# Five gate projections in 512-wide pairs, with new homes for two of the gate tiles, in a two-layer hybrid trunk kernel

## The chip, the core and the metric

The kernel runs on one core of a Trainium2 chip. A core has five engines with an instruction stream each: TensorE (PE in the profile) multiplies matrices and writes its sums into PSUM, VectorE (DVE) and ScalarE (ACT) do elementwise work and are the ones that read PSUM here, GpSimd (POOL) does a little elementwise work, and SyncE (SP) starts most of the transfers from memory. The engines run side by side and wait for each other by semaphores, each in the order of its own stream. The metric is the time of one execution on the device, in microseconds (us).

## What is computed

There are 256 positions of width 1024 and two layers. Each layer normalises its input, projects it by one weight matrix into ten pieces, runs three branches, multiplies each branch by a SiLU gate, projects the concatenation back and adds it to the input. A last normalisation ends the program. All is float32 (the kernel works with products of rounded halves, see below).

```python
def hybrid_layer(x, ...):
    hn = rms_norm(x, norm_gain)
    proj = einsum('bsd,de->bse', hn, w_in)
    a_q, a_k, a_v, a_g, b_x, b_g, c_q, c_k, c_v, c_g = split(proj)
    y_a = dilated_attention(rope(a_q), rope(a_k), a_v) * silu(a_g)     # width 512, 8 heads
    y_b = rg_lru_branch(b_x, ...) * silu(b_g)                          # width 256, a scan over time
    y_c = stick_breaking_attention(c_q, c_k, c_v) * silu(c_g)          # width 256, 4 heads
    y = concatenate([y_a, y_b, y_c])
    return x + einsum('bse,ed->bsd', y, w_out)
```

## The kernel before

**Precision by halves.** TensorE multiplies in a rounded float32 form, so each float operand is kept as a rounded half and a remainder: weights as `whi` and `wlo`, the normalised input as `xh` and `xl`. A product is whi·xh + whi·xl + wlo·xh. `xh` and `xl` lie side by side in one tile `xx`. The weights arrive in chunks of 256 output columns: `load_chunk` (L102) starts two transfers, then ACT rounds four pieces of 512 columns into `whi` (L115) and DVE subtracts four remainders into `wlo` (L117). `weights(l, c)` hands out a chunk and asks for the one two places on. Four chunks can be held at a time.

**Two ways to project a chunk.** `proj_b` (L326) computes the 256 outputs of a chunk in two halves of 128, for all 256 positions. Unpaired (L353, helper `mm3`, L225), both halves go into one PSUM bank, and each half is 24 matmuls with 256 columns: 8 of whi·xh, 8 of whi·xl, 8 of wlo·xh. Paired (L336 to L351), a half has a bank of its own: 8 matmuls with the 512 columns of `xx` (L344) give whi·xh and whi·xl side by side, and 8 with 256 columns (L341) add wlo·xh. Afterwards ACT copies the right part of the bank into a tile `low` (L347), and DVE adds it to the left part (L349) into `to`, a tile in SBUF that the caller names, or a scratch tile. The first half begins with its 512-wide matmuls, the second with its 256-wide ones. The table `PAIRED` (L46) says which chunks of which layer are paired: in before none of layer 0, and seven of layer 1.

**Banks.** The pool `pp` has three PSUM banks. A bank is free again when the instructions that read it are done. `at` has four others (tiles `s`), `yp` one (tile `y`).

**The order of the work around the gates.** The code of a layer from L654 on runs: the stick-breaking gate chunk CG; the turning of the softmaxed scores of dilated heads 0 to 3; the recurrence's gate chunk BG, between whose halves the function `third` stands (recurrence gates, stick-breaking values and their `emit_y`, values of dilated heads 0 to 3 into a `pp` bank that is kept as `y_c["y"]`, scores of heads 4 to 7); the recurrence's scan `lru_scan` and its `emit_y`; the softmax of heads 4 to 7; the first dilated gate AG; `emit_y` of heads 0 to 3, which frees the bank of `y_c["y"]`; the second dilated gate AG+1; and the output projection. `silu` (L423) applies the gate: in layer 0 DVE first scales the sums by the row norms (L413, reading the sums' bank), then ACT takes the sigmoid (L429) and DVE multiplies (L430). `emit_y` multiplies a branch by its gate (L434), rounds (L436, `yh`) and subtracts (L437, `yl`). The rows of `w_out` are packed in the order `yk`, so that block k of the products `ys` meets its weights.

**The output projection** (from L682) sums over eight blocks of `ys`, first blocks 0 to 3 (`ys[0]`: recurrence and stick-breaking) for four output tiles, then blocks 4 to 7. In layer 1 one output tile is started on a bank that still holds the leftover of AG+1 (`seeded`), into which ACT writes a part of the residual (L692).

PE's stream has the order of the code. The streams of the other engines are ordered by a scheduler when the program is built, so a row of the code may come later there than it stands. Names in the rows below: `pp_`, `s_`, `y_` are PSUM banks, `scr_` scratch tiles, `pr_` softmax probabilities, `den_` their denominators, `th_`, `it_`, `rt_`, `av_` tiles of the recurrence.

Of the kernel before, what the change touches and what calls it, by code (L numbers as in the profile page):

```python
# [9 lines left out]
F32 = mybir.dt.float32  # L10
# [5 lines left out]
P = 128  # L16
S = 256
# [25 lines left out]

CH_AV, CH_CV, CH_CQ, CH_CK, CH_BX, CH_CG, CH_BG, CH_AG, CH_O = 0, 2, 3, 4, 7, 10, 11, 12, 14
CH_AQ, CH_AK = (5, 8), (6, 9)
PAIRED = ((), (CH_CQ, CH_CK, CH_AQ[0], CH_AK[0], CH_BX, CH_AQ[1], CH_AK[1]))  # L46


@with_exitstack
def trunk_kernel(ctx: ExitStack, tc: tile.TileContext, x, first_x, first, wpack, prm_d, gatew, gains, consts, rope, out):  # L50
# [6 lines left out]
    sb = ctx.enter_context(tc.tile_pool(name="sb", bufs=1))  # L57
    wk = ctx.enter_context(tc.tile_pool(name="wk", bufs=2))
    pp = ctx.enter_context(tc.tile_pool(name="pp", bufs=3, space=bass.MemoryType.PSUM))
# [3 lines left out]
    def bank(pool, tag):  # L63
        return pool.tile([P, 512], F32, name=tag, tag=tag)

    def scr(w):
        return wk.tile([P, 512], F32, name="scr", tag="scr", bufs=SCR)[:, 0:w]
# [3 lines left out]
    def dep(inst, on):  # L71
        tc.add_manual_dep(inst.ins, on.ins.name, nosync)
        return inst
# [3 lines left out]
    def table(name, behind=()):  # L77
        load = act.preload_act_table_set(name)  # L78
        for u in (*loaded["users"], *behind):
            dep(load, u)  # L80
        loaded["load"], loaded["users"] = load, []
# [6 lines left out]
    def v2(a, n=2):  # L88
        return a.rearrange("p (b t) -> p b t", b=n)
# [40 lines left out]
    def weights(l, c, ahead=AHEAD):  # L130
        ask(l, c, ahead)
        return ready.pop((l, c))
# [16 lines left out]
    for k in range(NK):  # L149
# [10 lines left out]
        w = st[:, S:1024]  # L160
# [67 lines left out]
    last = {}  # L228
# [82 lines left out]
    for l in range(L):  # L311
# [14 lines left out]
        def proj_b(c, mid=None, to=None, sc=1.0):  # L326
            pair = c in PAIRED[l]
            hi, lo = [a.rearrange("p (k c) -> p k c", c=256) for a in weights(l, c, AHEAD - 1 if mid else AHEAD)]
            if pair:
                flat = None if to is not None else scr(512)  # L330
                to = [v2(flat)[:, b, :] for b in range(2)] if to is None else to
            else:
                flat = bank(pp, "pp")
            for b in range(2):
                cs = slice(b * P, b * P + P)
                if pair:  # L336
                    ps = bank(pp, "pp")
                    seq = [(b ^ i, k) for i in range(2) for k in range(NK)]
                    for i, (is_lo, k) in enumerate(seq):
                        if is_lo:  # L340
                            pe.matmul(ps[:, 0:S], lo[:, k, cs], xh[:, k, :], start=i == 0, stop=i == len(seq) - 1,  # L341
                                      skip_group_check=True)
                        else:
                            pe.matmul(ps, hi[:, k, cs], xx[:, k].rearrange("p h t -> p (h t)"), start=i == 0,  # L344
                                      stop=i == len(seq) - 1, skip_group_check=True)
                    low = wk.tile([P, S], F32, name="low", tag="low", bufs=2)
                    act.activation(low, ps[:, S:2 * S], AF.Copy, scale=sc)  # L347
                    if sc == 1.0:
                        dve.tensor_add(to[b], ps[:, 0:S], low)  # L349
                    else:  # L350
                        dve.scalar_tensor_tensor(to[b], ps[:, 0:S], sc, low, ALU.mult, ALU.add)  # L351
                else:
                    mm3(flat[:, b * 256:(b + 1) * 256], [lambda k, a=a: a[:, k, cs] for a in (hi, lo)],  # L353
                        [lambda k, a=a: a[:, k, :] for a in (xh, xl)], range(NK), b == 0, True, True)
                if b == 0 and mid:
                    mid()
                    ask(l, c)
            return flat

        def proj_to(dst, c, mid=None, sc=1.0):  # L360
            if l > 0 and c in PAIRED[l]:
                proj_b(c, mid, [dst[:, b, :] for b in range(2)], sc)
# [40 lines left out]
        vc = sb.tile([P, NT, 256], F32, name="vc", tag="vc")  # L403
# [19 lines left out]
        def silu(dst, ps):  # L423
            sg = v2(scr(512))
            src = v2(ps)
            if l == 0:
                src = v2(scr(512))
                scaled(src, ps)
            tab(sg, src, AF.Sigmoid)  # L429
            dve.tensor_mul(dst, src, sg)  # L430

        def emit_y(src, gate, k0, n):
            dst = v2(scr(n * S), n)
            dve.tensor_mul(dst, src, gate)  # L434
            yh, yl = [v[:, k0 % 4:k0 % 4 + n, :] for v in ys[k0 // 4]]
            act.activation(yh, dst, AF.Copy)  # L436
            dve.tensor_sub(yl, dst, yh.bitcast(F32))  # L437
# [4 lines left out]
        def values(vt, wts, h0, y=None):  # L442
            y = bank(yp, "y") if y is None else y
            for p in (0, 2):
                for s0, o in ((0, 0), (1, 128)):
                    for i in (p, p + 1):
                        hr, _, hs = head(h0 + i)
                        pe.matmul(y[hr, p * 128 + o:p * 128 + 256], vt[:, s0, hs], wts[i][s0],  # L448
                                  start=s0 == 0, stop=s0 == 1)
            return v2(y)  # L450
# [122 lines left out]
        rt = sb.tile([P, 2, S], F32, name="rt", tag="rt")  # L573
        it = sb.tile([P, 2, S], F32, name="it", tag="it")
        th = sb.tile([P, 2, S], F32, name="th", tag="th")
        bg = sb.tile([P, 2, S], F32, name="bg", tag="bg")
        cg = sb.tile([P, 2, S], F32, name="cg", tag="cg")
# [61 lines left out]
        sw_t, sw_heads = turned_tile()  # L639
# [20 lines left out]

        def third():
            lru_gates()
            emit_y(values(vc, sw_heads, 0), cg, 2, 2)
            y_c["y"] = values(va, pts, 0, bank(pp, "pp"))
            y_c["s"] = dil_scores(4)

# [1 line left out]
        y_half(1)  # L668
        table(LN_EXP)
        lru_scan()  # L670
        emit_y(rt, bg, 0, 2)
        dil_softmax(y_c["s"])
        ag = sb.tile([P, 4, S], F32, name="ag", tag="ag")
        ps = proj_b(CH_AG)
        table(SIGM)
        silu(ag[:, 0:2, :], ps)
        emit_y(y_c["y"], ag[:, 0:2, :], 4, 2)
        seeded = proj_b(CH_AG + 1)
        silu(ag[:, 2:4, :], seeded)
        table(LN_EXP)  # L680

        def out_mm(ps, w, t, half, ks, first, last, c0=0, c1=512, skip=False):  # L682
            v = [a.rearrange("p (k c) -> p k c", c=512) for a in w]
            ts_ = slice(t * P, t * P + P)
            mm3(ps, [lambda k, a=a: a[:, k, ts_] for a in ys[half]],
                [lambda k, a=a: a[:, k, c0:c1] for a in v], ks, first, last, skip)

        o_ps = {}
# [4 lines left out]
        for n2 in range(2):  # L693
            w = weights(l, CH_O + n2)
            for t in range(NT):
                if l > 0 and (t, n2) == (1, 1):
                    tail = [(bank(yp, "y")[:, 0:LATE], 0, LATE), (seed, LATE, 512)]
                    for ps, c0, c1 in tail[::-1]:
                        out_mm(ps, w, t, 0, range(4), c0 == 0, False, c0, c1, c0 > 0)
                    continue  # L700
                o_ps[t, n2] = bank(at, "s") if (t, n2) == (0, 0) else bank(pp, "pp")
                out_mm(o_ps[t, n2], w, t, 0, range(4), True, False)
                if (t, n2) == (0, 0):
                    y_c["p"] = dil_transposes(4)
                if (t, n2) == (0, 1):
                    emit_y(values(va, y_c["p"], 4), ag[:, 2:4, :], 6, 2)
# [57 lines left out]
def _pack_weights(w_in, w_out):  # L764
    wp = np.empty((L, NCH, P, 2048), np.float32)
    narrow = ((CH_CV, 3072), (CH_BX, 2048), (CH_BG, 2304), (CH_AG, 1536), (CH_AG + 1, 1792), (CH_CG, 3328),
              (CH_CQ, 2560), (CH_CK, 2816), (CH_AQ[0], 0), (CH_AQ[1], 256), (CH_AK[0], 512), (CH_AK[1], 768))
    yk = (4, 5, 6, 7, 0, 1, 2, 3)
    for l in range(L):
        wi = w_in[l].reshape(NK, P, 3584)  # L770
        for h in range(2):
            wp[l, CH_AV + h] = wi[4 * h:4 * h + 4, :, 1024:1536].transpose(1, 0, 2).reshape(P, 2048)
        for c, col in narrow:
            blk = wi[:, :, col:col + 256]
            if c in CH_AQ + CH_AK:
                blk = blk.reshape(NK, P, 4, 2, 32).transpose(0, 1, 3, 2, 4).reshape(NK, P, 256)
            wp[l, c] = blk.transpose(1, 0, 2).reshape(P, 2048)
        wo = w_out[l].reshape(NK, P, D)
        for h in range(2):
            for n in range(2):  # L780
                blk = np.stack([wo[k, :, n * 512:n * 512 + 512] for k in yk[4 * h:4 * h + 4]])
                wp[l, CH_O + 2 * h + n] = blk.transpose(1, 0, 2).reshape(P, 2048)
    return wp
# [56 lines left out]
```

## Time and profile before

| what | us |
|---|---|
| median of 3 runs (lowest, highest) | 245.55 (245.23, 247.58) |
| the profiled execution, its own time | 246.08 |
| its span, from first to last instruction | 244.2 |
| DVE busy, of the span | 195.7 (80%) |
| ACT busy, of the span | 171.5 (70%) |

The views of the profile that are quoted below have these forms. A row of the timeline has a start, a duration, an engine, the source line, the operation, output<-input, the shape and a count: equal instructions that follow each other are one row. Matmuls overlap at their ends, so what a row costs PE is the time from its start to the next row's start. A row of the list of waits has the waiting engine and line, whom it waited for, the total, the count and the longest. A row by windows has the window, its length, the busy time (and count) of PE, PE's weight loads, DVE, ACT and POOL, the clock granted to TensorE as a share of the full one, the share of DMA, and GB/s.

### The profile page before, as it was taken

Reading aid. Unit: us, or ns where it says so; the run is one execution under the profiler, and the core shown is the slowest. Engines: PE = TensorE matmul, PEld = TensorE weight load, DVE = VectorE, ACT = ScalarE, POOL = GpSimd, SP = SyncE. Lnnn points to the kernel's source line nnn. Section 1 sums busy time; section 2 is a strip of 40 time slices with the busy share of each in tenths; the row PEclk is TensorE's granted clock in tenths of the full one; section 3 lists DMA queues with packets and bytes.
Section 4 is the critical chain, followed back from the end, with each engine's and each line's share of the span. In section 5 each row is a group of like instructions: output and inputs, shape, how many; then the busy total and the mean of one; then the engine's idle time right before and its main releaser. Section 6 shows DMA issues by size and latency. Waiting matters only on the chain.

```text
span 244.2 us, 4755 instructions
## 1 busy us (share of the span) xinstructions
PE 237.5 (97%) x1747; PEld 212.1 (87%) x1747; DVE 195.7 (80%) x468; ACT 171.5 (70%) x372; POOL 11.3 (5%) x43
## 2 busy tenths in 40 slices
PE   8999999999999999999999999999999999999991
PEld 4788999999998899878888888888889889987881
DVE  4794789999999888986594675999999967885262
ACT  4669989628688499974663775876579749993143
POOL 0037100002000000000000000000010000000000
PEclk9999999999999999999999999999999999999997
DMA  7989989455836832277358388606470762000013
GB/s 211 395 262 386 381 274 309 167 192 182 274 120 217 300 112 77 87 217 274 113 154 262 114 268 269 212 15 191 156 215 27 238 257 86 0 3 0 0 53 121
DMA packets 14038, 43.90 MB, mean 180 GB/s; under 512 B 1728, under 2 KB 3008, under 8 KB 14016
## 3 DMA queue, kind: packets, MB, share of 16 engines
q1 hardware_dynamic: 13248, 42.43, 51.6%
q10 hardware_dynamic: 576, 0.66, 0.7%
q0 software_dynamic: 192, 0.52, 0.7%
q8 instruction: 14, 0.23, 0.4%
q14 instruction: 8, 0.07, 0.1%
HBM read 42.03 MB, written 1.05 MB: 176 GB/s over the span
## 4 chain that ended last, share of the span: by engine, by line
PE 94%; DMA 3%; ACT 1%; SPq 0%; issue 0%; DVE 0%; DVEq 0%
PE pp L225 48%; PE pp L344 10%; PE s L225 9%; PE pp L341 6%; PE s L181 4%; PE s L484 3%; DMA st<-first 3%; PE y L448 2%; PE pp L383 2%; PE s L537 2%; PE pp L181 2%; PE s L464 1%; PE y L225 1%; PE pp L448 1%; PE s L596 1%; PE s L273 1%
## 5 line engine op out<-in xcount | busy, mean ns | idle before, releaser
L117 DVE TENSOR_TENSOR wlo<-st,whi 128x512 fp32r<-128x512 f32 x128 | 81.6, 682 | 9.1 <-ACT whi L115 8.7
L115 ACT ACTIVATE whi<-st 128x512 fp32r<-128x512 f32 x130 | 72.5, 627 | 13.0 <-PE pp L225 6.8
L225 PE MATMUL pp<-xx,whi 128*128 128x256 f32 x480 | 63.6, 285 | 0.0
L225 PEld LDWEIGHTS pp<-xx,whi 128*128 128x128 f32 x480 | 59.7, 191 | 1.3 <-issue 0.3
L225 PE MATMUL pp<-xx,wlo 128*128 128x256 f32 x240 | 33.7, 283 | 0.0
L225 PEld LDWEIGHTS pp<-xx,wlo 128*128 128x128 f32 x240 | 31.0, 192 | 0.0
L344 PE MATMUL pp<-xx,whi 128*128 128x512 f32 x112 | 27.2, 392 | 0.0
L344 PEld LDWEIGHTS pp<-xx,whi 128*128 128x128 f32 x112 | 20.5, 188 | 3.9
L84 ACT ACTIVATE pr<-scr,mn 128x128 f32<-128x128 f32 (+1 forms) x32 | 14.1, 442 | 6.6 <-DVE mn L544 6.6
L78 ACT ACT_TABLE_LOAD x13 | 16.7, 1283 | 1.9 <-PEq L833 1.7
L341 PEld LDWEIGHTS pp<-xx,wlo 128*128 128x128 f32 x112 | 14.5, 191 | 1.0 <-ACT scr L84 0.3
L341 PE MATMUL pp<-xx,wlo 128*128 128x256 f32 x112 | 15.3, 285 | 0.0
L225 PE MATMUL pp<-whi,yh 128*128 128x512 f32 (+1 forms) x48 | 13.3, 382 | 0.0
L225 PE MATMUL pp<-wlo,yh 128*128 128x512 f32 (+1 forms) x48 | 12.8, 372 | 0.0
L225 PE MATMUL pp<-whi,yl 128*128 128x512 f32 (+1 forms) x48 | 12.8, 372 | 0.0
L181 PE MATMUL s<-whi,xx 128*128 128x512 f32 (+1 forms) x36 | 9.8, 392 | 0.4 <-ACT whi L167 0.4
L436 ACT ACTIVATE yh<-scr 128x512 fp32r<-128x512 f32 x8 | 5.1, 632 | 7.2 <-DVE scr L434 7.1
L225 PEld LDWEIGHTS pp<-whi,yl 128*128 128x128 f32 x48 | 8.6, 188 | 1.6
L225 PEld LDWEIGHTS pp<-wlo,yh 128*128 128x128 f32 x48 | 8.6, 188 | 1.6
L225 PEld LDWEIGHTS pp<-whi,yh 128*128 128x128 f32 x48 | 8.3, 188 | 1.6 <-issue 0.3
L544 DVE CUSTOM_DVE_ANT_0 scr<-s,con 128x128 f32<-128x128 f32 (+1 forms) x32 | 9.2, 350 | 0.0
L347 ACT ACTIVATE low<-pp 128x256 f32<-128x256 f32 x14 | 5.3, 378 | 5.5 <-PE pp L344 4.7
(188 smaller groups left out, 368.4 us busy)
## 6 DMA issues: line engine op xcount, KB each, us to landing
st<-w_pack SPq DMA_DIRECT2D x66, 512.0 KB, 5.3
st<-first SPq DMA_DIRECT2D x7, 512.0 KB, 6.3
xres<-x_in SPq DMA_DIRECT2D x4, 256.0 KB, 6.9
gw_t<-gate_w SPq DMA_DIRECT2D x2, 256.0 KB, 6.4
gn<-gains SPq DMA_DIRECT2D x2, 256.0 KB, 5.7
xs<-xc POOLq DMA_DIRECT2D x4, 128.0 KB, 4.3
gf<-gains SPq DMA_DIRECT2D x2, 256.0 KB, 6.0
out<-st ACTq DMA_DIRECT2D x2, 192.0 KB, 2.6
```

Of the source, the lines that this page charges most:

```text
L78: load = act.preload_act_table_set(name)
L84: i = dep(act.activation(*a, **k), loaded["load"])
L115: split[l, c] = act.activation(h, part, AF.Copy)
L117: dve.tensor_sub(r, part, h.bitcast(F32))
L181: pe.matmul(ps[t][:, c0:c1], a[:, k, t * P:(t + 1) * P], b, start=k == 0 and all(m[0] is not ps for m in seq[:i]), stop=k == NK - 1 and al ...
L225: pe.matmul(ps, a(k), b(k), start=first and i == 0, stop=last and i == len(seq) - 1, skip_group_check=skip)
L341: pe.matmul(ps[:, 0:S], lo[:, k, cs], xh[:, k, :], start=i == 0, stop=i == len(seq) - 1, skip_group_check=True)
L344: pe.matmul(ps, hi[:, k, cs], xx[:, k].rearrange("p h t -> p (h t)"), start=i == 0, stop=i == len(seq) - 1, skip_group_check=True)
L347: act.activation(low, ps[:, S:2 * S], AF.Copy, scale=sc)
L448: pe.matmul(y[hr, p * 128 + o:p * 128 + 256], vt[:, s0, hs], wts[i][s0], start=s0 == 0, stop=s0 == 1)
L484: pe.transpose(tp[:, i * P:(i + 1) * P], tiles[h0 + h][:, j * P:(j + 1) * P], ident)
L544: dve.tensor_tensor_reduce(xs[:, cs], sps[h][:, cs], nmask[:, cs], -0.125, 3e38, ALU.add, ALU.min, mn[:, t:t + 1])
```

## The change

The change pairs five more chunks: CG, BG, AG and AG+1 of layer 1, and AG+1 of layer 0. In layer 1 the sums of AG go into a tile `agf` in the place that the gate of the stick-breaking branch (`cg`) had, and AG is called ahead of the softmax of heads 4 to 7. The leftover bank of layer 1 (`seeded`) is now the one of the second half of AG+1. The stick-breaking product becomes block 0 and 1 of `ys`, the recurrence's block 2 and 3 (with `w_out` packed to suit), and the first four blocks of an output tile are multiplied in two groups of two blocks.

```diff
-PAIRED = ((), (CH_CQ, CH_CK, CH_AQ[0], CH_AK[0], CH_BX, CH_AQ[1], CH_AK[1]))
+PAIRED = ((CH_AG + 1,), (CH_CQ, CH_CK, CH_AQ[0], CH_AK[0], CH_BX, CH_AQ[1], CH_AK[1], CH_CG, CH_BG, CH_AG, CH_AG + 1))
...
                 if pair:
-                    ps = bank(pp, "pp")
+                    ps = last["bank"] = bank(pp, "pp")
...
             lru_gates()
-            emit_y(values(vc, sw_heads, 0), cg, 2, 2)
+            emit_y(values(vc, sw_heads, 0), cg, 0, 2)
...
         lru_scan()
-        emit_y(rt, bg, 0, 2)
+        emit_y(rt, bg, 2, 2)
+        ag = sb.tile([P, 4, S], F32, name="ag", tag="ag")
+        ps = None
+        if CH_AG in PAIRED[l]:
+            agf = sb.tile([P, 2, S], F32, name="agf", tag="cg")
+            proj_b(CH_AG, None, [agf[:, b, :] for b in range(2)])
+            ps = agf.rearrange("p b t -> p (b t)")
         dil_softmax(y_c["s"])
-        ag = sb.tile([P, 4, S], F32, name="ag", tag="ag")
-        ps = proj_b(CH_AG)
+        ps = proj_b(CH_AG) if ps is None else ps
         table(SIGM)
         silu(ag[:, 0:2, :], ps)
         emit_y(y_c["y"], ag[:, 0:2, :], 4, 2)
         seeded = proj_b(CH_AG + 1)
         silu(ag[:, 2:4, :], seeded)
+        if CH_AG + 1 in PAIRED[l]:
+            seeded = last["bank"]
...
                 o_ps[t, n2] = bank(at, "s") if (t, n2) == (0, 0) else bank(pp, "pp")
-                out_mm(o_ps[t, n2], w, t, 0, range(4), True, False)
+                for ks in ((0, 1), (2, 3)):
+                    out_mm(o_ps[t, n2], w, t, 0, ks, ks[0] == 0, False)
...
-    yk = (4, 5, 6, 7, 0, 1, 2, 3)
+    yk = (6, 7, 4, 5, 0, 1, 2, 3)
```

PE in layer 0, before: AG (`pp_1352`), AG+1 in one bank (`pp_1425`), the first output tile.

```order
L225 MATMUL pp_1352<-xx_81,whi_1042 128x256 x16
L225 MATMUL pp_1352<-xx_81,wlo_1043 128x256 x8
L225 MATMUL pp_1425<-xx_81,whi_1247 128x256 x16
L225 MATMUL pp_1425<-xx_81,wlo_1248 128x256 x8
L225 MATMUL pp_1425<-xx_81,whi_1247 128x256 x16
L225 MATMUL pp_1425<-xx_81,wlo_1248 128x256 x8
L225 MATMUL s_1494<-whi_1338,yh_1130 128x512 x4
```

The same place with the change: AG+1 has a bank for each half, `pp_1426` and `pp_1446`.

```order
L225 MATMUL pp_1352<-xx_81,whi_1042 128x256 x16
L225 MATMUL pp_1352<-xx_81,wlo_1043 128x256 x8
L344 MATMUL pp_1426<-xx_81,whi_1247 128x512 x8
L341 MATMUL pp_1426<-xx_81,wlo_1248 128x256 x8
L341 MATMUL pp_1446<-xx_81,wlo_1248 128x256 x8
L344 MATMUL pp_1446<-xx_81,whi_1247 128x512 x8
L225 MATMUL s_1486<-whi_1338,yh_1130 128x512 x2
```

When `pp_1446` is asked for, two of the three banks are taken by `y_c["y"]` and by `pp_1426`, so it is the bank of `pp_1352`, and its first matmul waits for the DVE instruction that reads `pp_1352`.

DVE in layer 0, before, from the recurrence's scan to that reader (L413) and on.

```order
L618 SCALAR_TENSOR_TENSOR rt_329<-av_1293,it_330 128x256 x2
L557 TENSOR_SCALAR pr_1323<-pr_1323,den_1324 128x128
L434 TENSOR_TENSOR scr_1305<-rt_329,bg_332 128x512
L557 TENSOR_SCALAR pr_1323<-pr_1323,den_1324 128x256
L555 RECIPROCAL den_1331<-den_1331 128x2
L413 SCALAR_TENSOR_TENSOR scr_1403<-pp_1352,rb_289 128x512
L557 TENSOR_SCALAR pr_1330<-pr_1330,den_1331 128x128
L437 TENSOR_TENSOR yl_1131<-scr_1305,yh_1130 128x512
```

The same with the change.

```order
L618 SCALAR_TENSOR_TENSOR rt_329<-av_1293,it_330 128x256 x2
L557 TENSOR_SCALAR pr_1324<-pr_1324,den_1325 128x128
L434 TENSOR_TENSOR scr_1305<-rt_329,bg_332 128x512
L557 TENSOR_SCALAR pr_1324<-pr_1324,den_1325 128x256
L555 RECIPROCAL den_1332<-den_1332 128x2
L413 SCALAR_TENSOR_TENSOR scr_1403<-pp_1352,rb_289 128x512
L557 TENSOR_SCALAR pr_1331<-pr_1331,den_1332 128x128
L437 TENSOR_TENSOR yl_1131<-scr_1305,yh_1130 128x512
```

The reader of `pp_1352` stands in the same row of DVE's stream in both, behind the recurrence's scan.

ACT in layer 1, before, from the rounding of the second output chunk (`whi_2821`) and BG's sigmoid (L84) to the recurrence's logarithm (`th_1848`).

```order
L115 ACTIVATE whi_2821<-st_2823 128x512 x2
L84 ACTIVATE scr_2699<-pp_2546 128x512
L78 ACT_TABLE_LOAD
L84 ACTIVATE av_2705<-rt_1846,c8_285 128x256 x2
L84 ACTIVATE pr_2721,den_2722<-scr_2645,mn_2646 128x128
L84 ACTIVATE pr_2721,den_2722<-scr_2645,mn_2646 128x256
L84 ACTIVATE pr_2728,den_2729<-scr_2649,mn_2650 128x128
L84 ACTIVATE pr_2728,den_2729<-scr_2649,mn_2650 128x256
L84 ACTIVATE th_1848<-scr_2709,tiny_281 128x512
```

The same with the change: `low_2672` is of BG's second half, `low_2730` and `low_2750` are of AG's halves.

```order
L347 ACTIVATE low_2672<-pp_2655 128x256
L115 ACTIVATE whi_2789<-st_2791 128x512 x2
L84 ACTIVATE scr_2675<-scr_2530 128x512
L78 ACT_TABLE_LOAD
L84 ACTIVATE av_2681<-rt_1838,c8_285 128x256 x2
L347 ACTIVATE low_2730<-pp_2713 128x256
L84 ACTIVATE pr_2753,den_2754<-scr_2625,mn_2626 128x128
L84 ACTIVATE pr_2753,den_2754<-scr_2625,mn_2626 128x256
L84 ACTIVATE pr_2760,den_2761<-scr_2629,mn_2630 128x128
L84 ACTIVATE pr_2760,den_2761<-scr_2629,mn_2630 128x256
L84 ACTIVATE th_1840<-scr_2685,tiny_281 128x512
L347 ACTIVATE low_2750<-pp_2733 128x256
```

The three copies stand among the recurrence's steps and the exponentials, and BG's sigmoid now reads a tile that DVE fills (`scr_2530`) in place of the bank.

## The prediction

> **What bounds the kernel now.** I read the engines' shares on the page first, then PE's list of waits, then PE's timeline around the changed chunks, and only then the timelines of DVE and ACT there.
>
> ```profile
> PE 237.5 (97%) x1747; PEld 212.1 (87%) x1747; DVE 195.7 (80%) x468; ACT 171.5 (70%) x372; POOL 11.3 (5%) x43
> ```
>
> ```profile
> PE y L147 <- DVE cold L135: 1.2, 1, 1.2
> PE s L181 <- ACT whi L167: 0.4, 1, 0.4
> ```
>
> PE is busy for 97% of the span, and its whole list of waits is two rows, both from the first ten microseconds. From there to the output PE goes from matmul to matmul without a hole. So the kernel has one price list. A microsecond less of PE work is a microsecond gained, a microsecond in which PE waits is a microsecond lost, and nothing later can give it back, since there is no later wait that it could shorten. Work on ACT and DVE costs nothing until PE waits for it.
>
> **What pairing saves.** PE's timeline has the same chunk size in both forms: AG+1 of layer 0, unpaired, and a chunk of layer 1 that is paired already.
>
> ```profile
> 91.66 2.08 PE L225 MATMUL pp<-xx,whi 128*128 128x256 f32 x16
> ...
> 97.42 1.09 PE L225 MATMUL s<-whi,yh 128*128 128x512 f32 x4
> ...
> 144.23 3.82 PE L344 MATMUL pp<-xx,whi 128*128 128x512 f32 x16
> 147.88 2.08 PE L341 MATMUL pp<-xx,wlo 128*128 128x256 f32 x16
> 149.80 3.82 PE L344 MATMUL pp<-xx,whi 128*128 128x512 f32 x16
> ```
>
> From start to start the unpaired chunk takes 97.42 - 91.66 = 5.76 us for 48 matmuls, 120 ns each. The paired one takes 149.80 - 144.23 = 5.57 us: 16 wide ones in 3.65 (228 ns each) and 16 narrow ones in 1.92. The same columns pass through the array; a wide matmul saves only about 11 ns against two narrow ones. That is 0.19 us per chunk, and a paired half is 1.83 + 0.96 = 2.79 us.
>
> [...]
>
> Layer 1, from PE's timeline (the row at 189.93 ends CG, the one at 202.31 begins AG, the one at 213.83 ends AG+1):
>
> ```profile
> 184.07 2.17 PE L225 MATMUL pp<-xx,whi 128*128 128x256 f32 x16
> ...
> 189.93 1.48 PE L484 MATMUL s<-con,pr 128*128 128x128 f32 x12
> ...
> 202.31 2.08 PE L225 MATMUL pp<-xx,whi 128*128 128x256 f32 x16
> ...
> 213.83 1.09 PE L225 MATMUL s<-whi,yh 128*128 128x512 f32 x4
> ```
>
> CG takes 5.86 us and will take 5.57: 0.29 saved. BG's halves stand among other work and save half of 0.19 each: 0.19. AG and AG+1 take 11.52 and will take 11.14: 0.38. Layer 1 saves 0.86 us, at the least nothing and at the most 1.2 (four chunks at CG's 0.29).
>
> **What pairing costs in layer 0.** A pair needs two banks where one did. The second half of AG+1 gets the bank of AG's sums, and those are read by DVE's L413, which stands behind the recurrence's scan. DVE's timeline there:
>
> ```profile
> 93.39 0.69 DVE L616 TENSOR_TENSOR it<-it,th 128x512 f32<-128x512 f32 x1 [0.54 <-ACT th L84]
> ...
> 95.48 0.68 DVE L434 TENSOR_TENSOR scr<-rt,bg 128x512 f32<-128x512 f32 x1
> ...
> 96.42 0.67 DVE L413 SCALAR_TENSOR_TENSOR scr<-pp,rb 128x512 f32<-128x512 f32 x1
> 97.01 0.27 DVE L557 TENSOR_SCALAR pr<-pr,den 128x128 f32<-128x128 f32 x1
> ```
>
> AG is finished on PE at 91.66, but its sums are read from 96.42 to 97.09, since DVE works through its stream in order and the scan ahead of L413 waits for ACT's exponential of `th`. In before nobody needed this bank so soon: all of AG+1 went into another one. Now PE does the first half of AG+1 from 91.66 to 94.45 and then needs the bank. Nothing ahead of L413 is touched by the change, so it still ends at 97.09. PE waits 2.6 us and does the second half until 97.13 + 2.87 = 100.0 (its first group after a pause is taken 0.08 longer). AG+1 ended at 97.42 before, so layer 0 loses 2.6 us, its 0.19 of saving already counted. The bounds are narrow, since all rows exist: 2.4 if the bank is given up with the next DVE row at 97.01 and the half takes 2.79; 2.9 if the handover costs 0.3. Everything behind waits for PE and moves along. ACT's and DVE's two copies and two adds are done while PE waits or has its next matmuls.
>
> **What pairing costs in layer 1.** Four chunks bring eight ACT copies and eight DVE adds. The question is whether a bank or a `yh` comes too late. The tightest place is the first half of AG+1, which needs the bank of AG's first half. ACT's timeline, the price of a copy, and DVE's row behind the recurrence's exponentials `av`:
>
> ```profile
> 184.36 0.37 ACT L347 ACTIVATE low<-pp 128x256 f32<-128x256 f32 x1
> ```
>
> ```profile
> 201.55 1.16 ACT L115 ACTIVATE whi<-st 128x512 fp32r<-128x512 f32 x2 [2.66 <-PE pp L225]
> 202.61 0.58 ACT L84 ACTIVATE scr<-pp 128x512 f32<-128x512 f32 x1
> 203.21 1.28 ACT L78 ACT_TABLE_LOAD   x1
> 204.50 0.91 ACT L84 ACTIVATE av<-rt,c 128x256 f32<-128x256 f32 x2
> ```
>
> ```profile
> 205.44 0.69 DVE L612 TENSOR_TENSOR scr<-av 128x512 f32<-128x512 f32 x1 [0.98 <-ACT av L84]
> ```
>
> On the clock of before, less what CG and BG save (0.48), BG ends on PE at 201.83. Its copy begins about 0.3 later (the copy at 184.36 follows a PE handover near 184.07) and takes 0.26 to the next start, an estimate from its 0.37 less the overlap of neighbouring rows: 202.4. Behind it the two roundings take 1.06 (201.55 to 202.61), the sigmoid 0.6, the table 1.29: `av` begins at 205.35, 0.85 later than before. DVE's L612 follows 0.94 behind, at 206.3, takes 0.6, and then the add that frees the bank takes 0.4: 207.3. PE wants the bank at 201.83 + 5.57 = 207.40. That fits by 0.1 us, so I take 0.1 for waits in layer 1, between 0 and 0.6 (a bank late by half a microsecond, a shade more elsewhere). The recurrence's `yh` is late by some 1.2 us in all, but the reordered output projection covers it: its first six matmuls (1.4 us at 228 ns) now multiply stick-breaking blocks, which are long there, where before the first one needed the recurrence.
>
> Edits with one answer. Splitting the first blocks of an output tile into two groups leaves the number and size of its matmuls. The leftover bank only changes its name. `agf` takes the place of `cg`, whose last reader is the product before AG. The order of SP's and POOL's transfers stays the same, so calling AG ahead of the softmax moves no load.
>
> **The sum.** -0.86 + 2.6 + 0.1 = +1.8 us. The profiled execution took 246.08 us (span 244.2) and would take 247.9. It stood 0.5 above the median of 245.55, on which I put the forecast: 247.4 us, +0.7%.
>
> **The rivals.** *Slower: the wait takes TensorE's clock with it.* The end of the run shows how the granted clock answers to idleness: PE's last row, and three windows behind it.
>
> ```profile
> 238.48 0.64 PE L225 MATMUL pp<-whi,yl 128*128 128x256 f32 x4
> ```
>
> ```profile
> 241.00:241.10 0.10, 0.00 (x0) 0.00 (x0) 0.00 (x0) 0.00 (x0) 0.00 (x0) 1.00 0.00 0
> 241.10:241.20 0.10, 0.00 (x0) 0.00 (x0) 0.00 (x0) 0.00 (x0) 0.00 (x0) 0.83 0.00 0
> 241.20:241.30 0.10, 0.00 (x0) 0.00 (x0) 0.00 (x0) 0.00 (x0) 0.00 (x0) 0.50 0.00 0
> ```
>
> The last matmul ends at 239.12 and the clock is halved at 241.17, after 2.05 us. The wait in layer 0 is 2.6 us, so it can be long enough. The beginning shows how long slow matmuls last:
>
> ```profile
> 1.19 3.17 PE L147 MATMUL y<-cold 128*128 128x512 bf16 x7 [1.19 <-DVE cold L135]
> 4.13 1.19 PE L181 MATMUL s<-whi,xx 128*128 128x256 f32 x4
> 5.13 0.63 PE L181 MATMUL pp<-whi,xx 128*128 128x256 f32 x2
> 5.55 0.69 PE L181 MATMUL s<-whi,xx 128*128 128x256 f32 x4
> 6.08 0.40 PE L181 MATMUL pp<-whi,xx 128*128 128x256 f32 x2
> ```
>
> At 4.13 four matmuls take 1.00 us (250 ns each), at 5.55 they take 0.53: full speed comes some 4.3 us after the first matmul. Half speed for 4.3 us loses at most 2.1 us, less if it starts within the wait. I take 1.5 (0.8 to 2.1): 247.35 + 1.5 = 248.9 us, +1.3%. It decides from a pause of about 2 us. [...]
>
> [...]
>
> *The pause does not come, only the saving.* If AG's sums left their bank by 94.45, layer 0 would save 0.19 and the total be -1.0: 244.6 us, -0.4%. For it speaks that the PE rows of pairing are certain; against it the row at 96.42, 2 us too late. It would need L413 to move ahead of the scan in DVE's stream, which it doesn't.
>
> *Layer 1 waits more.* If the chain on ACT slips by another 0.5 us at each half of AG+1 and at the recurrence's `yh`, up to 1 us is lost: 248.3 us. The 0.1 of room speaks for it, and that later chunks have more room against.
>
> **How the numbers follow.** The sum as it stands: 0.50. The clock falls: 0.38. Layer 1 waits more: 0.08. No pause: 0.04. About 1% (2.46 us, so 243.1 and 248.0) is what a measurement of this kernel can tell from no change. The sum lies 0.65 below the upper bound, more than the width of its terms, so it counts as the same but for 0.04; the clock case counts as slower but for 0.09, where the loss is small or only some executions have it; the third is split evenly. Slower: 0.04 + 0.29 + 0.04 = 0.37. Of the case without a pause, half (0.02) is put to faster, for savings larger than the rows show. The rest, 0.61, is the same. The forecast is the likeliest case, 247.4. Its own range is 247.0 to 248.0; the range over the cases runs from 246.5 (a shorter pause) to 249.3 (the clock falls at a middling to high price).
>
> **What would show it.** PE's list of waits should have a row of about 2.6 us in layer 0 at L341, released by DVE at L413, and PE's row before it should be the eight narrow matmuls of the first half. Chunks CG, AG and AG+1 of layer 1 should take 5.57 us each. A second PE wait, at L344 in layer 1, would be the third rival. The windows behind the pause show the granted clock: 1.00 is the forecast, 0.50 the first rival. The forecast is wrong if there is no wait at L341, or if it is far from 2.6 us, or if the output projection of layer 1 waits.

## The result, and the profile after

| | before | after |
|---|---|---|
| median of the runs | 246.0 us (6 runs, 245.23 to 247.58) | 249.64 us (6 runs, 248.33 to 252.26) |
| profiled execution, its span | 246.08 us, 244.2 us | 248.44 us, 246.5 us |
| ratio after to before, 95% interval | | 1.0124 [1.0092, 1.0156] |

The change makes the kernel slower by 1.2%, about 3.05 us of 246.0. The forecast was 247.4 (246.5 to 249.3): 246.0 + 3.05 = 249.05 lies near its upper end, and the median of all six runs, 249.64, a little above. The ratio leaves out the run of 252.26, which stands over 1.5% above the fastest of its kernel; only the counts by clock below include it.

The other five runs of after fall into two groups by the mean granted clock of TensorE: 248.33 and 248.44 us at 1.000, and 249.38, 249.9 and 250.65 us at 0.993, 0.993 and 0.988. The means are 248.39 and 249.98, so in these five runs the lower clock goes with 1.6 us more. The profiled execution is one of the first group.

First the engines' shares of after, then PE's list of waits (what waits, for which releaser: us in all, times, the longest).

```profile
PE 236.4 (96%) x1667; PEld 207.2 (84%) x1667; DVE 199.5 (81%) x478; ACT 174.6 (71%) x382; POOL 10.6 (4%) x43
```

```profile
PE pp L341 <- DVE scr L413: 2.5, 1, 2.5
PE s L181 <- ACT xx L161: 1.2, 1, 1.2
PE y L147 <- DVE cold L135: 1.2, 1, 1.2
```

PE does 80 matmuls fewer and is busy for 1.1 us less, yet the span is 2.3 us longer. The list has one row without a counterpart in before, 2.5 us at L341 for DVE's L413; the other two are from the first ten microseconds (L181 waits 0.8 longer there than in before, for another releaser). PE's timeline of after in layer 0 shows where it stands, and DVE's what held it (start, us, engine, line, operation, out<-in, count, idle time before with its releaser).

```profile
86.25 2.08 PE L225 MATMUL pp<-xx,whi 128*128 128x256 f32 x16
...
92.01 2.00 PE L344 MATMUL pp<-xx,whi 128*128 128x512 f32 x8
93.85 1.11 PE L341 MATMUL pp<-xx,wlo 128*128 128x256 f32 x8
97.50 1.22 PE L341 MATMUL pp<-xx,wlo 128*128 128x256 f32 x8 [2.54 <-DVE scr L413]
98.56 2.00 PE L344 MATMUL pp<-xx,whi 128*128 128x512 f32 x8
100.40 0.62 PE L225 MATMUL s<-whi,yh 128*128 128x512 f32 x2
...
240.81 0.64 PE L225 MATMUL pp<-whi,yl 128*128 128x256 f32 x4
```

```profile
94.47 1.27 DVE L618 TENSOR_TENSOR_SCAN rt<-av,it 128x256 f32<-128x256 f32 x2
...
95.83 0.69 DVE L434 TENSOR_TENSOR scr<-rt,bg 128x512 f32<-128x512 f32 x1
...
96.77 0.67 DVE L413 SCALAR_TENSOR_TENSOR scr<-pp,rb 128x512 f32<-128x512 f32 x1
```

The first half of AG+1 is done at 94.96, and the second starts at 97.50, just as L413 ends at 97.44. DVE works all through the pause; what PE waits for is not work of the change, but a row of DVE's stream that stands where it stood. AG+1 takes 100.40 - 92.01 = 8.39 us in place of 5.76: 2.63 lost.

The runs' times scatter by some two microseconds, in the kernel before too. Part of that arises early: in the ten profiles AG of layer 0 starts between 85.52 and 87.26, and in the latest of them (layer 1 only, below) PE waits 0.92 us at 29.89 for weights whose load is late. So the traces are compared below over a fixed stretch: from the start of AG in layer 0 to the start of PE's last row. Before, AG started in this row:

```profile
85.90 2.08 PE L225 MATMUL pp<-xx,whi 128*128 128x256 f32 x16
```

The stretch is 238.48 - 85.90 = 152.58 us before and 240.81 - 86.25 = 154.56 after: +1.98. Layer 0 has 2.63 of it, so the rest of the stretch gives back 0.65. PE's timeline of after in layer 1:

```profile
185.17 4.01 PE L344 MATMUL pp<-xx,whi 128*128 128x512 f32 x16
189.01 2.06 PE L341 MATMUL pp<-xx,wlo 128*128 128x256 f32 x16
...
192.76 1.48 PE L484 MATMUL s<-con,pr 128*128 128x128 f32 x12
...
208.73 3.86 PE L344 MATMUL pp<-xx,whi 128*128 128x512 f32 x16
212.43 2.08 PE L341 MATMUL pp<-xx,wlo 128*128 128x256 f32 x16
214.34 2.00 PE L344 MATMUL pp<-xx,whi 128*128 128x512 f32 x8
216.18 0.62 PE L225 MATMUL s<-whi,yh 128*128 128x512 f32 x2
...
217.54 0.62 PE L225 MATMUL s<-whi,yh 128*128 128x512 f32 x2
```

A group of 16 wide matmuls that waits for nothing shows as 3.82 us (in before's layer 1). The group at 185.17, whose second eight begin CG, shows 4.01; the one at 208.73, whose second eight begin AG+1, shows 3.86. The weight loads' list of waits names both places:

```profile
PEld pp L344 <- DVE q L349: 0.3, 1, 0.3
PEld pp L344 <- DVE agf L349: 0.2, 1, 0.2
```

So CG's first half comes 0.2 us late because DVE's add (L349) still reads the bank that it wants (3.84 us to the next row in place of 3.65).

### The profile page after: what moved, and what is told of

The parts are those of the page before. It is cut to its first block, busy times and chain, and to the rows that moved or that the text cites. A ratio compares the mean times of both kernels' runs of the same rounds, so it can differ in the third digit from the quotient of the medians.

```text
span 246.5 us, 4611 instructions
## 1 busy us (share of the span) xinstructions
PE 236.4 (96%) x1667; PEld 207.2 (84%) x1667; DVE 199.5 (81%) x478; ACT 174.6 (71%) x382; POOL 10.6 (4%) x43
## 4 chain that ended last, share of the span: by engine, by line
PE 89%; ACT 3%; DVE 3%; DMA 2%; issue 0%; SPq 0%; DVEq 0%
PE pp L225 33%; PE pp L344 17%; PE pp L341 9%; PE s L225 9%; PE s L181 4%; PE s L484 3%; PE y L448 2%; DMA st<-first 2%; PE pp L383 2%; PE s L537 2%; PE pp L181 2%; PE s L464 1%; PE y L225 1%; PE pp L448 1%; ACT whi L115 1%; PE s L596 1%
## 5 line engine op out<-in xcount | busy, mean ns | idle before, releaser
L344 PE MATMUL pp<-xx,whi 128*128 128x512 f32 x192 | 47.0, 393 | 0.0
L225 PE MATMUL pp<-xx,whi 128*128 128x256 f32 x320 | 42.2, 285 | 0.0
L344 PEld LDWEIGHTS pp<-xx,whi 128*128 128x128 f32 x192 | 34.9, 188 | 7.0 <-DVE q L349 0.3
L225 PEld LDWEIGHTS pp<-xx,whi 128*128 128x128 f32 x320 | 39.7, 192 | 0.6 <-issue 0.3
L341 PE MATMUL pp<-xx,wlo 128*128 128x256 f32 x192 | 26.1, 285 | 2.5 <-DVE scr L413 2.5
L341 PEld LDWEIGHTS pp<-xx,wlo 128*128 128x128 f32 x192 | 24.9, 191 | 4.3 <-DVE scr L413 2.7
L225 PE MATMUL pp<-xx,wlo 128*128 128x256 f32 x160 | 22.4, 283 | 0.0
L84 ACT ACTIVATE pr<-scr,mn 128x128 f32<-128x128 f32 (+1 forms) x32 | 14.1, 443 | 6.6 <-DVE mn L544 6.6
L347 ACT ACTIVATE low<-pp 128x256 f32<-128x256 f32 x24 | 8.9, 375 | 9.2 <-PE pp L344 8.4
L225 PE MATMUL pp<-whi,yh 128*128 128x512 f32 (+1 forms) x48 | 14.1, 382 | 0.0
L225 PE MATMUL pp<-wlo,yh 128*128 128x512 f32 (+1 forms) x48 | 13.7, 372 | 0.0
L225 PE MATMUL pp<-whi,yl 128*128 128x512 f32 (+1 forms) x48 | 13.6, 371 | 0.0
L181 PE MATMUL s<-whi,xx 128*128 128x512 f32 (+1 forms) x36 | 9.4, 379 | 1.3 <-ACT xx L161 1.2
```

What stands on the lines that cost most here:

```text
L84: i = dep(act.activation(*a, **k), loaded["load"])
L181: pe.matmul(ps[t][:, c0:c1], a[:, k, t * P:(t + 1) * P], b, start=k == 0 and all(m[0] is not ps for m in seq[:i]), stop=k == NK - 1 and al ...
L225: pe.matmul(ps, a(k), b(k), start=first and i == 0, stop=last and i == len(seq) - 1, skip_group_check=skip)
```

## The experiments

In all of them `after` is the kernel with the change, and times are medians. The kernel before stood at 246.29 us beside the first four (25 runs) and at 245.96 beside the other four (26 runs). "Stretch" is the one above, from one profile of each kernel, against before's 152.58.

| kernel | us (range, runs) | ratio to before [95%] | stretch against before |
|---|---|---|---|
| layer 1 only | 245.92 (244.91 to 246.79, 12) | 0.9983 [0.996, 1.0007] | -0.65 |
| layer 0 only | 250.63 (247.99 to 251.6, 6) | 1.0164 [1.012, 1.0208] | +4.19 |
| other bank | 245.01 (244.28 to 247.68, 12) | 0.9963 [0.9934, 0.9992] | -0.85 |
| pause filled | 248.09 (247.45 to 249.54, 8) | 1.0083 [1.0055, 1.0112] | +1.94 |
| pause half filled | 247.69 (247.26 to 249.09, 9) | 1.0072 [1.0046, 1.0099] | +1.94 |
| longer pause | 252.2 (251.54 to 253.55, 6) | 1.0259 [1.022, 1.0298] | +6.39 |
| no reordering | 245.58 (244.78 to 248.61, 12) | 0.9992 [0.9961, 1.0024] | -0.33 |
| two other banks | 245.05 (244.38 to 246.96, 12) | 0.9971 [0.994, 1.0001] | -1.00 |

**The two layers apart.** The theory: all of the loss is in layer 0's pair. The rival: layer 1's copies and adds cost something too. One kernel drops the pair of layer 0,

```diff
-PAIRED = ((CH_AG + 1,), (CH_CQ, ...
+PAIRED = ((), (CH_CQ, ...
```

> AG+1 of layer 0 unpaired again, all else as in the changed kernel. Theory A (the pause of PE in layer 0 is the whole loss, with what the clock adds to it): no PE wait in layer 0, layer 1 keeps its saving of 0.6 us, so 0.6 us below the kernel before, about 245.4 us. Rival C (layer 1 loses too, through bank waits or later work on ACT): equal to the kernel before or slower, 246.0 us or more.

and the other is the kernel before with that pair alone.

```diff
-PAIRED = ((), (CH_CQ, CH_CK, CH_AQ[0], CH_AK[0], CH_BX, CH_AQ[1], CH_AK[1]))
+PAIRED = ((CH_AG + 1,), (CH_CQ, CH_CK, CH_AQ[0], CH_AK[0], CH_BX, CH_AQ[1], CH_AK[1]))
```

> The kernel before with AG+1 of layer 0 paired and nothing else. Theory A: a PE wait of about 2.5 us at L341 in layer 0, released by DVE L413, and AG+1 ends 2.6 us later than in the kernel before; runs without a fall of the clock take 2.6 us more (about 248.6 us), runs with one 1 to 2 us more than that, so a median of about 250 us. Rival C: less than 2 us over the kernel before, since part of the loss would belong to layer 1.

Layer 1 alone shortens the stretch by 0.65 us (239.19 - 87.26 = 151.93), as much as the rest of after's stretch gives back; the times alone cannot show it, since the ratio does not exclude 1. Layer 0 alone makes the kernel slower by 1.6%, and its stretch grows by 4.19 us (243.11 - 86.34 = 156.77). That is 1.56 more than the 2.63 of after. PE's timeline of this kernel has the same pause, and then something else:

```profile
92.10 2.00 PE L344 MATMUL pp<-xx,whi 128*128 128x512 f32 x8
93.94 1.11 PE L341 MATMUL pp<-xx,wlo 128*128 128x256 f32 x8
97.59 1.48 PE L341 MATMUL pp<-xx,wlo 128*128 128x256 f32 x8 [2.53 <-DVE scr L413]
98.87 3.34 PE L344 MATMUL pp<-xx,whi 128*128 128x512 f32 x8
102.05 1.09 PE L225 MATMUL s<-whi,yh 128*128 128x512 f32 x4
```

AG+1 takes 102.05 - 92.10 = 9.95 us, so all of the 4.19 stands here. Its last eight wide matmuls take 102.05 - 98.87 = 3.18 us, where they took 1.84 in after's profile. The windows of the same kernel (stretch, its length, busy time of PE, PEld, DVE, ACT and POOL with counts, then the granted clock) give the reason:

```profile
98.30:98.40 0.10, 0.10 (x3) 0.10 (x2) 0.10 (x2) 0.10 (x1) 0.00 (x0) 0.72 0.00 0
98.60:101.60 3.00, 3.00 (x10) 2.42 (x9) 2.72 (x5) 1.68 (x4) 0.00 (x0) 0.50 0.00 0
101.70:101.80 0.10, 0.10 (x1) 0.06 (x1) 0.00 (x0) 0.00 (x0) 0.00 (x0) 0.71 0.00 0
```

A window in which the clock changes shows a mean of 1.00 and 0.50: 0.72 over 0.1 us puts the fall at 98.34, and 0.71 the return at 101.76. So the clock is granted at half for 3.41 us, and the fall comes 0.75 us after PE has started again. This is the prediction's first rival, seen in a profile. In after's own profile the window behind the pause stands at full clock:

```profile
98.00:102.00 4.00, 4.00 (x23) 3.39 (x22) 3.70 (x8) 3.60 (x9) 0.00 (x0) 1.00 0.00 0
```

With the same 2.5 us of pause the clock thus falls in some executions only. The mean clock tells which: before's 51 runs beside the experiments stand at 0.994 to 1.000 (the halving behind the last matmul explains that much; the profile in which it begins at 241.17 has 0.994). Below that are 4 of after's 6 runs and 5 of this kernel's 6: 9 of 12. Its one run without the fall took 247.99, the others 249.32 to 251.6. Three of the nine rest on the last digit alone: they stand at 0.993, are not profiled, and took 249.38, 249.9 and 249.32.

**The pause taken away.** If the bank is the only cause, a bank from another pool takes away the pause and the clock's fall together. The pool `at` has one free at that time.

```diff
-                    ps = last["bank"] = bank(pp, "pp")
+                    ps = last["bank"] = bank(at, "s") if (l, b) == (0, 1) else bank(pp, "pp")
```

> The changed kernel, but in layer 0 the second half of AG+1 takes a bank of the pool of the s tiles, which is free there, in place of the bank of AG's sums. Theory A: no PE wait in layer 0, both layers keep their saving (0.2 and 0.6 us), about 0.8 us below the kernel before, 245.2 us, and runs no wider apart than those of the kernel before. Rival (the pairing itself is late for another reason, such as the later add for the third turning): PE waits elsewhere in layer 0 and the time stays above 246 us.

PE's timeline has no pause any more, the second half (now `s`) following the first:

```profile
92.84 2.00 PE L344 MATMUL pp<-xx,whi 128*128 128x512 f32 x8
94.68 1.12 PE L341 MATMUL pp<-xx,wlo 128*128 128x256 f32 x8
95.63 1.12 PE L341 MATMUL s<-xx,wlo 128*128 128x256 f32 x8
96.59 2.00 PE L344 MATMUL s<-xx,whi 128*128 128x512 f32 x8
```

The stretch is 238.81 - 87.08 = 151.73, 0.85 under before: the 0.65 of layer 1 and some 0.2 of this pair. None of its 12 runs has a clock under 0.994. At 245.01 us, 0.9963 [0.9934, 0.9992], it is well under after and a little under before, by an interval that only just excludes 1.

**The clock apart from the pause.** To see whether the pause costs the clock because PE is idle, PE is given work in it whose result nobody reads: ten wide matmuls into a bank of the pool `yp`, ahead of the second half.

```diff
+                    if (l, b) == (0, 1):
+                        idle = bank(yp, "y")
+                        for _ in range(10):
+                            pe.matmul(idle, hi[:, 0, cs], xx[:, 0].rearrange("p h t -> p (h t)"), start=True, stop=True)
```

> The changed kernel with ten more 512-wide matmuls (10 x 0.228 = 2.28 us) into an unused bank between the halves of AG+1 in layer 0, so that PE works where it waited; they change no result. Theory A with the clock: the end does not move in the runs without a fall, about 248.2 us, and no run shows a fall within the program, so the median drops from 249.6 to about 248.2 us and the runs lie within 1 us. Rival B (the longer runs of the changed kernel have nothing to do with PE's idleness): median and width as for the changed kernel, 249.6 us and 248.3 to 252.3.

A second kernel has `range(5)` there.

> As the run with ten added matmuls, with five (1.14 us): about 1.4 us of the pause stay. The pause itself costs the same as in the changed kernel (2.0 us more than the kernel before, about 248.2 us). [...] Rival B2 (any pause makes the clock fall, more often the longer it is): some runs with a mean clock of 0.993 or less and 1.6 us more.

The wait for the bank stays (L417 and L345 are L413 and L341 of after), and PE's idle time shrinks to 0.2 us with ten and to 1.4 us with five. The row of the first, then of the second, from PE's lists of waits:

```profile
PE pp L345 <- DVE scr L417: 0.2, 1, 0.2
```

```profile
PE pp L345 <- DVE scr L417: 1.4, 1, 1.4
```

Both stretches are as long as in after's profile without the fall (+1.94 each, beside +1.98), so the added matmuls cost nothing and the second half starts when the bank comes. But of the 17 runs none has a clock under 0.994, and the medians are 248.09 and 247.69 where after has 249.64. Against before they lose 1.8 and 1.7 us, about the stretch and no more. So 2.5 us of idle PE can be enough to lose the clock, and 1.4 us were not in any of 9 runs.

**The pause lengthened.** The opposite: a bank is taken and released by a DVE row that stands late in DVE's stream, so that the second half waits longer.

```diff
                 if pair:
+                    if (l, b) == (0, 1):
+                        skipped = bank(pp, "pp")
+                        dve.memset(skipped[:, 0:1], 0.0)
```

> The changed kernel with the bank of AG's sums kept back until a small added memset on DVE, so that PE's pause in layer 0 grows from 2.5 to about 4.2 us. Theory A: 3.7 us more than the kernel before by the pause, and the clock falls in every run, with about 1.6 us each: about 251.5 us, all mean clocks 0.993 or less. Rival B: 3.7 us more and no more, about 250.0 us, falls as seldom as with 2.5 us.

PE's timeline (L344 and L347 are L341 and L344 of after), and the windows:

```profile
99.36 2.05 PE L344 MATMUL pp<-xx,wlo 128*128 128x256 f32 x8 [4.35 <-DVE pp L339]
101.21 3.61 PE L347 MATMUL pp<-xx,whi 128*128 128x512 f32 x8
104.62 0.84 PE L225 MATMUL s<-whi,yh 128*128 128x512 f32 x2
```

```profile
98.30:99.30 1.00, 0.00 (x0) 0.00 (x0) 1.00 (x4) 1.00 (x3) 0.00 (x0) 0.50 0.00 0
...
101.70:105.00 3.30, 3.30 (x9) 2.58 (x8) 1.44 (x4) 0.14 (x1) 0.00 (x0) 0.50 0.59 196
...
105.10:106.00 0.90, 0.90 (x6) 0.72 (x5) 0.69 (x2) 0.90 (x3) 0.00 (x0) 1.00 0.80 246
```

The pause is 1.81 us longer, and the stretch grows by 245.27 - 86.30 - 154.56 = 4.41 against after's: the other 2.6 are the clock, at half from about 98.26 to 105.08, two times 3.4 us. All six runs have a clock of 0.993 or less, four of them, the profiled one among these, 0.980 to 0.982; the two at 0.993 are the shortest (251.54 and 251.73).

**The reordered projection.** The prediction held that `yh` of the recurrence comes late in layer 1 and that the six matmuls on stick-breaking blocks cover it. This is the other-bank kernel with before's order of the blocks.

```diff
-            emit_y(values(vc, sw_heads, 0), cg, 0, 2)
+            emit_y(values(vc, sw_heads, 0), cg, 2, 2)
...
-        emit_y(rt, bg, 2, 2)
+        emit_y(rt, bg, 0, 2)
...
-                for ks in ((0, 1), (2, 3)):
-                    out_mm(o_ps[t, n2], w, t, 0, ks, ks[0] == 0, False)
+                out_mm(o_ps[t, n2], w, t, 0, range(4), True, False)
...
-    yk = (6, 7, 4, 5, 0, 1, 2, 3)
+    yk = (4, 5, 6, 7, 0, 1, 2, 3)
```

> The kernel with the bank of the s pool (no pause), but the blocks of the products and the first half of the output projection in the order of the kernel before. If the reordering covers the recurrence's late yh: a PE wait of 0.3 to 0.6 us at the first output matmuls of layer 1 and that much more than the run with the s bank, 245.3 to 245.6 us. If it has no part in the time: no such wait and the same as that run, 245.0 us.

Its list of waits and PE's timeline show the wait that the change avoids:

```profile
PE s L225 <- ACT yh L436: 0.2, 1, 0.2
```

```profile
211.05 2.00 PE L344 MATMUL pp<-xx,whi 128*128 128x512 f32 x8
213.25 1.19 PE L225 MATMUL s<-whi,yh 128*128 128x512 f32 x4 [0.20 <-ACT yh L436]
```

The matmuls at 211.05 end their 1.84 at 212.89, and the projection starts at 213.25. Over the stretch the kernel is 0.52 us longer than the other-bank kernel; 0.36 of it stands at this place, and 0.14 in the output tile behind it (216.12 - 213.25 = 2.87, where the other-bank kernel takes 216.92 - 214.19 = 2.73). The times do not tell the two apart (0.9992 and 0.9963, with overlapping intervals). One of its 12 runs, 248.61 us, has a clock of 0.993 without a pause of this kind. A fall inside the program would give that, but so would a halving behind the last matmul that begins some 0.2 us earlier than in before's profile (an estimate from its 0.994 and 241.17); it stays open.

**CG's bank.** CG's late first half is given a bank of the pool `at` too.

```diff
+                    ps = last["bank"] = bank(at, "s") if (l, b) == (0, 1) or (l, c, b) == (1, CH_CG, 0) else bank(pp, "pp")
```

> The kernel with the bank of the s pool, and the first half of CG in layer 1 in a bank of that pool too. In the changed kernel this half waited some 0.15 us for the add of the second query chunk. If that is why CG saved 0.13 us and not 0.29: PE's timeline gets 0.15 us shorter there, about 0.2 us under the run with the s bank, 1.0 us under the kernel before. If not: the same as that run.

```profile
184.02 1.98 PE L344 MATMUL s<-xx,whi 128*128 128x512 f32 x8
...
187.75 2.01 PE L344 MATMUL pp<-xx,whi 128*128 128x512 f32 x8
189.59 1.48 PE L484 MATMUL s<-con,pr 128*128 128x128 f32 x12
```

In PE's timeline CG now takes 189.59 - 184.02 = 5.57 us, what a pair takes that waits for nothing. The stretch is 0.15 shorter than with the one other bank; the times (245.05 and 245.01) cannot show so little.

## Why the prediction was right or wrong

- **PE is the bound, and pairing saves 0.19 us a chunk.** Right. The paired CG takes 5.57 without a wait, and the two kernels without the pause gain what their pairs save.
- **Layer 0's pair waits for L413: 2.6 us lost.** Right in place, releaser and size: 2.54 us of pause, 2.63 lost. The kernel with another bank shows that the bank is the cause.
- **Layer 1 saves 0.86.** The mechanism was right, one term was too large: CG was put at 0.29 and saved 0.13. In before's timeline the last eight wide matmuls of the chunk ahead of CG start in this row,

```profile
182.21 2.00 PE L344 MATMUL pp<-xx,whi 128*128 128x512 f32 x8
```

  and from there to CG's end it took 189.93 - 182.21 = 7.72; after it takes 192.76 - 185.17 = 7.59. The prediction weighed late banks at AG and AG+1, and not at CG's first half, which follows a chunk that was paired already and whose add was still at the bank. Before's list of the weight loads' waits has this wait too, at the same place:

```profile
PEld pp L225 <- DVE q L349: 0.3, 1, 0.3
```

  Without it the eight wide matmuls and CG would take 1.83 + 5.76 = 7.59 before and 1.83 + 5.57 = 7.40 after, so they were 0.13 late before and are 0.19 late after. The 0.29 counted the removal of a wait that pairing does not remove; pairing gave its 0.19, and the bank took back 0.06. With another bank CG saves its 0.29.
- **Waits of 0.1 in layer 1, tightest at AG+1's first half.** Right: the row at 208.73 shows 0.04 us of it. The stretch from CG's end on saves 23.90 - 23.42 = 0.48 (213.83 - 189.93 before, 216.18 - 192.76 after); the terms were 0.19 + 0.38 - 0.1.
- **The late `yh` is covered.** Right. ACT writes it in after from 215.86 on,

```profile
215.86 0.63 ACT L436 ACTIVATE yh<-scr 128x512 fp32r<-128x512 f32 x1
```

  while PE begins the projection at 216.18 and needs it in its seventh matmul at 217.54. It is done at 216.49, 0.31 behind the start of the projection, where the prediction had 1.2. With the old order PE waits for it.
- **The sum of +1.8.** It was +1.98 in the profile of after, whose clock did not fall.
- **The likeliest case.** This is the step that failed. "The clock falls: 0.38" was the usual case, 9 runs in 12, and the forecast was built on the other one. Its cause was right: without the pause, or with PE at work in much of it, no run shows the fall (one of 65 is open). Its price came out right as well (1.5 predicted; 1.56 in the profile of layer 0 alone, 1.6 between after's two groups of runs), in part by luck, since it was taken from 4.3 us at half speed and the fall lasts 3.41. The 2.05 us came from one end of a run; three other profiles show 4.78 to 5.01 us there (last section), so the "about 2 us" from which the prediction let the case decide was its estimate from one profile. With the clock case chosen the forecast would have been 248.9. By the runs the loss is then 1.98 + 1.6 = 3.6 us; after's three runs with the fall that the ratio counts stand 249.98 - 246.0 = 4.0 over before's median. Another 0.45 of the distance is the starting point: the forecast stands on 245.55, and the kernel before has 246.0 over six runs.

## What to carry to other kernels

Splitting a chunk's sums over two banks is to be paid in banks: find who reads the older bank, where that row stands in its engine's stream, and compare it with when the matmuls want the bank. In this kernel, which TensorE bounds, a pause of 2.54 us cost its length (2.63 us) and, in 9 runs of 12 (with those of layer 0 alone), the clock too (half for 3.41 us in the profile of layer 0 alone), and the second price, 1.56 us, was over half of the first. Before giving up such an edit, look for a bank of another pool that is idle at that time: one changed line took the ratio here from 1.0124 [1.0092, 1.0156] to 0.9963 [0.9934, 0.9992].

## What the hardware showed

In the two profiles in which the clock falls at the pause, it was granted at half for 3.41 us (layer 0 alone, 98.34 to 101.76) and for 6.82 us (longer pause, 98.26 to 105.08). The pauses began at 95.05 and 95.01, so the falls came 3.29 and 3.25 us behind their beginning. In the first kernel that was 0.75 us after PE had started again at 97.59; in the second PE still stood until 99.36. Full clock came back 4.17 and 5.72 us after PE had started again.

In four profiles read for it the clock falls behind the last matmul too, in before 2.05 us behind it. The rows that hold this fall, in the kernels of layer 0 alone, of the whole change and of layer 1 alone:

```profile
248.50:248.60 0.10, 0.00 (x0) 0.00 (x0) 0.00 (x0) 0.00 (x0) 0.00 (x0) 0.66 0.00 0
```

```profile
246.20:246.40 0.20, 0.00 (x0) 0.00 (x0) 0.00 (x0) 0.00 (x0) 0.00 (x0) 0.73 0.00 0
```

```profile
244.80:244.90 0.10, 0.00 (x0) 0.00 (x0) 0.00 (x0) 0.00 (x0) 0.00 (x0) 0.72 0.00 0
```

They put the falls at 248.53, 246.29 and 244.84. PE's last matmuls end at 243.75, 241.45 and 239.83 (the ends of matmuls are modelled in the profile), so the clock stayed full for 4.78, 4.84 and 5.01 us of idleness, where it was 2.05 in before. In these profiles the length of the idleness alone does not tell when the clock falls.

Within the program it fell, by the runs' mean clocks (below 0.994), in none of 8 with 0.2 us of idleness left at the pause, in none of 9 with 1.4, in 9 of 12 with 2.5 (the kernels of the whole change and of layer 0 alone), and in all 6 with 4.35. What spared the other three of the twelve, after's profile among them, stays open.
